# Two products of a projection merged into one of 512 columns, and gate and up columns as units of their own

## The chip, the cores and the metric

The kernel runs on one NeuronCore of a Trainium2 chip. The metric is the device time of one execution in microseconds (us). PE is TensorE (matrix products), PEld its weight loads, DVE is VectorE, ACT is ScalarE, POOL is GpSimd, SP issues the loads of the weights.

## The reference

Two blocks run one after the other, each of two layers, on 256 tokens of width 1024, all in float32. Cut to what matters:

```python
def first_block(x, ...):                       # sequence x alone
    for l in range(2):
        h = rms_norm(x, norm1_g[l])
        rq, rk, rv, rg, sq, sk, sv = split(h @ w_in[l])          # 7 x 512 columns
        ret = head_group_norm(chunk_retention(rotary(rq), rotary(rk), rv)) * silu(rg)
        sb = head_rms_norm(stick_breaking(sq, sk, sv))
        x = x + concat(ret, sb) @ w_out[l]
        h = rms_norm(x, norm2_g[l])
        x = x + (silu(h @ w_gate[l]) * (h @ w_up[l])) @ w_down[l]  # 2816 columns
    return rms_norm(x, final_g)

def second_block(x, c, ctx, c_ctx, ...):       # sequences x and h = ctx, 256 tokens each
    for l in range(2):
        mod_x, mod_h = silu(c) @ w_mod[l] + b_mod[l], silu(c_ctx) @ w_mod[l] + b_mod[l]
        x, h = ffn_sublayer(x, mod_x, 0, ...), ffn_sublayer(h, mod_h, 0, ...)
        # three kinds of mixing between x and h, then w_out
        x, h = ffn_sublayer(x, mod_x, 2, ...), ffn_sublayer(h, mod_h, 2, ...)   # h only if l == 0
    return x

def ffn_sublayer(s, mod, j, g_pre, g_post, wg, wu, wd):
    y = rmsnorm(s, g_pre) * (1 + mod[3*j+1]) + mod[3*j]
    return s + 0.5 * mod[3*j+2] * rmsnorm((silu(y @ wg) * (y @ wu)) @ wd, g_post)
```

## The kernel before, in words

Weights are streamed from memory in pieces of 512 KB (`Gran`), loaded once by SP into `raw` and split into two float32r parts, high and low, in the tile `hl`: for each half of a piece ACT casts the high part and DVE subtracts it to get the low one. Five pieces are held at a time (`R_SLOTS`). Activations are held in the same two parts: `y[:, 0]` is the high part of a normed input, `y[:, 1]` the low one, each as eight slices k of 128 features by 256 tokens. A product is three float32r products that add up in PSUM (`mm3`, L522): weight high by input high, weight high by input low, weight low by input high.

- `proj` (L527) makes two times 128 output features for 256 tokens, in one PSUM bank of two halves: for each slice k, three products of 256 columns for the one piece and three for the other, 48 in all. In block 2's feed-forward and in block 1's, the pair is a gate column and an up column (`col`, L818); in block 1's input projection it is two neighbouring pieces (`rope`, L1098, and `plain`, L1117). Block 2's input projection (`attn2`) uses `proj` too.
- What follows a product is its tail on ACT and DVE. For a column in block 2: silu of the gate half (ACT, tile `sg`), times the up half (DVE), then a split into the parts of `a` (ACT, DVE). In block 1 the factor of each token (`rfac`) is multiplied in first, on both halves (DVE, tile `gu`).
- `row_units` (L760) multiplies two such columns with a 256-row piece of the down weight, in products of 512 columns: into four PSUM banks that are held for the whole feed-forward (`mm_f`), or, for sequence h, into one bank at a time that DVE adds up in SBUF (`mm_r`, `fo`). There are 22 columns and 11 pairs of rows to a feed-forward.
- Ahead of a projection the normed input is turned around by PE (`mm_y`, 16 transposes) and written to `y` by ACT and DVE, slice by slice (`pre_units`, L604, `pre_raw`, L668).
- The modulation of block 2 (`mod_units`, L977) is worked out on DVE beside all this: `modacc` adds up `modraw` times a factor, 1024 columns at a time, loaded by POOL; a total is turned by PE (`mm_t`) and reduced by DVE (`modt`).

The order on PE, DVE and ACT is set by a planner (`run`, L263): it reckons when each instruction starts and ends from a table of costs, issues the products in the order in which they can start, the tails in the order in which they get ready, and puts the modulation wherever DVE is free. That order is fixed in the program; at run time each engine works through its own list and waits for what a step needs. A unit's first product may be ordered 3.5 us ahead of the end of the transposes' tail (`L_TR`).

Of the kernel before, what the change touches and what calls it, by code (L numbers as in the profile page):

```python
# [58 lines left out]
# constant table columns: always on chip, block 1's, block 2's  # L59
# [20 lines left out]
def const_tables():  # L80
    """Tables that depend on shapes alone."""
# [42 lines left out]
class Gran:  # L124
    """A 512 KB piece of a weight: loaded once, split into two float32r parts."""
# [10 lines left out]
# what a unit takes on PE, in ns, and the PSUM banks that it holds until its end  # L136
PE_NS = {"col": 5260, "proj": 5260, "rope1": 5260, "half1": 2630, "half2": 2630, "row": 1295, "row_add": 1295, "row_last": 1295,
# [3 lines left out]
BANKS = {"row": 0, "row_add": 1, "row_last": 0, "half2": 0, "happly": 2, "sc2": 2, "bapply": 2}  # L141
# [6 lines left out]
class Meter:  # L148
    """Reckons when the instructions of DVE and ACT begin and end. at, last: when what the next one needs is
    there, and the engine that it comes from."""  # L150

    def __init__(self):
        self.free = {"v": 0.0, "a": 0.0, "pe": 0.0}
        self.at, self.last = 0.0, None
        self.act_set = None
        self.spawned = []

# [5 lines left out]
    def spawn(self, gen):  # L163
        """gen goes on beside the tail that calls this"""
        self.spawned.append((gen, self.at, self.last))


class Engine:
    """PE, DVE or ACT: issues an instruction and reckons how long it takes."""
# [5 lines left out]
    def ns(self, op, args, kw):  # L175
# [33 lines left out]
class Chained:  # L209
    """DVE, for a short instruction that needs the one before it"""  # L210
# [25 lines left out]
class Tail:  # L236
# [26 lines left out]
def run(streams, grans, r_slots, raw_slots, load, split, meter):  # L263
    """Merges the streams and emits them, at the times that are reckoned: products in the order in which they
    can start, what follows them on DVE and ACT in the order in which it gets ready, and the splitting of
    weights (up to r_slots ahead) and the work on the modulation in between."""
# [28 lines left out]
    def runway():  # L295
        """the work for PE that needs no further piece of a weight; 1e9 if no stream waits for one after it"""
# [37 lines left out]
    def advance(x):  # L334
        meter.at, meter.last = x.at + (CHAIN if x.chained and x.last == "v" else 0.0), x.last
        nxt = next(x.gen, None)
        x.at, x.last = meter.at, meter.last
        u = x.unit
        take_spawned(u)
# [15 lines left out]
    while True:  # L355
        # the next product of each stream
# [102 lines left out]
def tile_two_blocks(ctx: ExitStack, tc, io, out):  # L459
# [40 lines left out]
    def t2k(shape, name):  # L500
        """a short-lived tile of 2 KB per partition"""
        return wk.tile(shape, F32, tag="t2k", name=name, bufs=4)
# [23 lines left out]

    def proj(ps, gs, y, ks=range(KT)):  # L527
        """feature-major: twice 128 output features by 256 tokens"""
# [5 lines left out]
    def proj_t(ps, gp, y, bs=(0, 1)):  # L534
        """token-major: 256 tokens by 256 output features"""
# [6 lines left out]
    def rsqrt_small(v, step=Chained):  # L542
        """v: SBUF [128, n], v > 0; gives v ** -0.5"""
# [24 lines left out]
    def bcast(rb, y):  # L568
        """rb[:, j*128 + t] = y[t, j] on every partition"""
# [4 lines left out]
    def sq_piece(c, b, e, src):  # L574
        """a part of the mean of squares: 512 features of 128 tokens"""
# [7 lines left out]
    def rstd_tok(c, bs, step=Chained, rest=None):  # L583
        """1 / root mean square of the tokens; to come after a yield"""
# [11 lines left out]
    def tail_of(*stages):  # L596
        """a tail from pairs of an engine and what to call"""
# [125 lines left out]
    def post_units(st, c, mode, u, apart=False, final=False, hard=False):  # L723
        """residual plus gate times the norm of what a sublayer gave; apart: one block of tokens at a time"""
# [35 lines left out]
    def row_units(st, c, gp, src_of, first, last, mode, deps, by_token=True):  # L760
        """two feature tiles times [256, 1024] of a weight, token-major: added to the residual ("res"),
        kept in PSUM ("ps") or added up in SBUF ("sb")"""
        u = None
        order = ((0, 0), (0, 1), (1, 0), (1, 1)) if last and by_token else ((0, 0), (1, 0), (0, 1), (1, 1))
        for n_, (b, e) in enumerate(order):
            def fn(b=b, e=e, n_=n_):
# [18 lines left out]
                def tail():  # L785
# [28 lines left out]
    def ffn(st, c, gg, gu, gd, mode, dep, pace, fac=None, by_token=True):  # L814
# [3 lines left out]
        def col(j):  # L818
            def fn():
                y = ytile[c]  # L820
                ps = mm_ps([P, 2, S], "mm_c")
                proj(ps, (gg[j], gu[j]), y)

                def tail():
                    if fac is None:
                        yield A
                        sg = t1k([P, S], "sg")
                        A.activation(sg, ps[:, 0, :], AF.Silu)
                        yield V
                        V.tensor_mul(sg, sg, ps[:, 1, :])  # L830
                    else:
                        yield V, fac["u"]
                        gu_ = t2k([P, 2, S], "gu")
                        sg = gu_[:, 0]
                        V.tensor_mul(gu_, ps, fac["rb"].unsqueeze(1).to_broadcast([P, 2, S]))
                        yield A
                        A.activation(sg, sg, AF.Silu)
                        yield V
                        V.tensor_mul(sg, sg, gu_[:, 1])
# [4 lines left out]
                    A.copy(hl[:, 0, :], sg)  # L844
                    yield V
                    V.tensor_sub(hl[:, 1, :], sg, hl[:, 0, :])
                    abox[j] = hl
                return tail
            cols[j] = st.add("col", fn, grans=[gg[j], gu[j]], deps=dep if j == 0 else ())
            pace.append(cols[j])  # L850

        def row(s):
            def src(k):
# [3 lines left out]
                             [(cols[2 * s + 1], 0.0)], by_token)  # L857

        for j in range(NJ):
            col(j)  # L860
# [13 lines left out]
    def load_rows(ap, n):  # L874
        """n pairs of pieces of 256 rows by 512 columns"""
# [3 lines left out]
    def load_mix(ap, n, kcols):  # L879
        """256-column pieces: pairs by rows for those in kcols, else by columns"""  # L880
# [64 lines left out]
    def start2():  # L945
# [993 lines left out]
```

## Time and profile before

| | |
|---|---|
| median of 3 runs | 2476.24 us (2475.47 to 2477.46) |
| span of the profiled execution | 2474.7 us |
| PE busy | 2415.5 us, 98% |
| DVE busy | 1731.8 us, 70% |
| ACT busy | 1092.0 us, 44% |
| granted TensorE clock, mean | 0.991 of full speed |

The span reaches from the first to the last instruction of the program. Almost all instructions bear the line L205, that of the helper that issues them, so they are told apart by their tiles, in the form out<-in: `mm_c<-y,hl` is a projection's product, `hl<-raw,hl` the second half of a weight's split. The float32 products that are not in two parts run as two passes each in the trace.

### The profile page before, as it was taken

How to read it: one execution, taken by the hardware profiler on the slowest of the kernel's cores; microseconds unless marked ns; L12 is line 12 of the kernel's file. 1: busy time of each engine (PE TensorE's matmuls, PEld its weight loads, DVE VectorE, ACT ScalarE, POOL GpSimd, SP SyncE). 2: the span in 40 equal slices, each digit the busy share in tenths (PEclk: the TensorE clock that was granted, in tenths of full speed). 3: DMA queues.
4: the chain of work that ended last, by engine and by line, in shares of the span. 5: the costliest groups of instructions: out<-in, count | busy, mean ns of one | idle time of the engine just before them, and what ended most of it. 6: DMA issues, size and time to landing. Idle time of an engine off the chain costs nothing.

```text
span 2474.7 us, 42550 instructions
## 1 busy us (share of the span) xinstructions
PE 2415.5 (98%) x16927; PEld 2231.3 (90%) x16927; DVE 1731.8 (70%) x3366; ACT 1092.0 (44%) x2337; POOL 99.1 (4%) x189
## 2 busy tenths in 40 slices
PE   7999999999999999999999999999999999997998
PEld 7999999999999999999669999999999998966997
DVE  5789867798879953755788994348899448486554
ACT  6654456544632222545566222236222226465443
POOL 1000000000001100000000100000110000000000
PEclk9999999999999999999999999999999999998999
DMA  6568655687656633622126762245665335322663
GB/s 218 161 209 246 202 161 164 186 254 222 195 173 200 188 93 99 177 88 86 60 94 204 214 188 79 87 125 180 195 203 172 95 94 175 90 86 77 189 193 121
DMA packets 461448, 386.31 MB, mean 156 GB/s; under 512 B 20512, under 2 KB 392548, under 8 KB 461248
## 3 DMA queue, kind: packets, MB, share of 16 engines
q1 hardware_dynamic: 437424, 299.67, 40.9%
q0 software_dynamic: 23648, 83.77, 10.4%
q8 instruction: 133, 2.18, 0.4%
q14 instruction: 67, 0.55, 0.1%
q10 hardware_dynamic: 176, 0.14, 0.0%
HBM read 382.43 MB, written 1.10 MB: 155 GB/s over the span
## 4 chain that ended last, share of the span: by engine, by line
PE 92%; DVE 5%; ACT 1%; issue 1%; DMA 1%; DVEq 0%; ACTq 0%
PE mm_c L205 59%; PE mm_f L205 18%; PE mm_r L205 7%; PE at_s L205 1%; PE mm_t L205 1%; DVE hl L205 1%; PE at_o L205 1%; PE at_t L205 1%; PE at_c L205 1%; DVE res L205 1%; PE mm_y L205 1%; DVE t L205 1%; PE st_rb L205 1%; DVE sx L205 0%; ACT sq L205 0%
## 5 line engine op out<-in xcount | busy, mean ns | idle before, releaser
L205 PE MATMUL mm_c<-y,hl 128*128 128x256 f32 x11616 | 1435.0, 284 | 8.7 <-DVE y L205 5.4
L205 PEld LDWEIGHTS mm_c<-y,hl 128*128 128x128 f32 x11616 | 1416.2, 192 | 23.8 <-DVE y L205 7.7
L205 ACT CAST hl<-raw 128x512 fp32r<-128x512 f32 x1128 | 646.9, 619 | 813.8 <-PE mm_c L205 460.1
L205 DVE TENSOR_TENSOR hl<-raw,hl 128x512 fp32r<-128x512 f32 x1128 | 735.1, 685 | 308.0 <-ACT hl L205 306.7
L205 PE MATMUL mm_f<-hl,a 128*128 128x512 f32 x1584 | 379.9, 392 | 0.0
L205 PEld LDWEIGHTS mm_f<-hl,a 128*128 128x128 f32 x1584 | 292.1, 188 | 58.1
L205 DVE SCALAR_TENSOR_TENSOR modacc<-modraw,sc,modacc 128x1024 f32<-128x1024 f32 x252 | 311.9, 1277 | 0.0
L205 PE MATMUL mm_r<-hl,a 128*128 128x512 f32 x792 | 192.9, 394 | 0.0
L205 ACT ACTIVATE sg<-mm_c 128x256 f32<-128x256 f32 x154 | 58.6, 380 | 303.2 <-PE mm_c L205 300.5
L205 PEld LDWEIGHTS mm_r<-hl,a 128*128 128x128 f32 x792 | 144.8, 188 | 28.1
L205 DVE TENSOR_TENSOR sg<-sg,mm_c 128x256 f32<-128x256 f32 x154 | 64.1, 416 | 151.4 <-ACT sg L205 150.9
L987 POOL DMA_DIRECT2D modraw<-in_w_mod_dram x144 | 77.0, 536 | 1060.2 <-DVE modacc L205 709.7
L205 PE MATMUL mm_f<-hl,o 128*128 128x512 f32 x480 | 119.4, 399 | 0.0
L205 PE MATMUL mm_c<-hl,y 128*128 128x256 f32 x912 | 113.7, 284 | 0.0
L205 PEld LDWEIGHTS mm_c<-hl,y 128*128 128x128 f32 x912 | 111.0, 192 | 0.3 <-issue 0.3
L205 PEld LDWEIGHTS mm_f<-hl,o 128*128 128x128 f32 x480 | 87.7, 188 | 22.9 <-issue 4.2
L205 DVE TENSOR_TENSOR fo<-fo,mm_r 128x512 f32<-128x512 f32 x120 | 81.9, 683 | 12.9 <-PE mm_r L205 11.5
L205 ACT CAST a<-sg 128x256 fp32r<-128x256 f32 x154 | 62.5, 406 | 31.9 <-DVE sg L205 31.9
L205 DVE TENSOR_REDUCE modt<-mm_t 128x4 f32<-128x512 f32 x72 | 49.3, 685 | 34.1 <-PE mm_t L205 34.0
L205 DVE TENSOR_TENSOR a<-sg,a 128x256 fp32r<-128x256 f32 x154 | 64.4, 418 | 8.0 <-ACT a L205 8.0
L205 DVE TENSOR_REDUCE sx<-at_s 128x1 f32<-128x512 f32 (+1 forms) x72 | 40.7, 596 | 31.7 <-PE at_s L205 31.3
L205 DVE TENSOR_TENSOR gu<-mm_c,rfac 128x512 f32<-128x512 f32 x44 | 30.4, 690 | 41.1 <-PE mm_c L205 40.9
(196 smaller groups left out, 1413.5 us busy)
## 6 DMA issues: line engine op xcount, KB each, us to landing
modraw<-in_w_mod_dram POOLq DMA_DIRECT2D x144, 512.0 KB, 4.8
raw<-in_ffn_w_down_dram SPq DMA_DIRECT2D x100, 512.0 KB, 4.1
raw<-in_ffn_w_gate_dram SPq DMA_DIRECT2D x98, 512.0 KB, 4.7
raw<-in_ffn_w_up_dram SPq DMA_DIRECT2D x98, 512.0 KB, 3.8
raw<-in_w_in_dram SPq DMA_DIRECT2D x92, 512.0 KB, 4.7
raw<-in_w_gate_dram SPq DMA_DIRECT2D x44, 512.0 KB, 5.0
raw<-in_w_up_dram SPq DMA_DIRECT2D x44, 512.0 KB, 4.7
raw<-in_w_down_dram SPq DMA_DIRECT2D x44, 512.0 KB, 4.5
```

Source lines behind the costliest of these rows:

```text
L205: return f(*args, **kw)
L987: G.dma_start(M["raw"][g % len(M["raw"])], wm[k * P:(k + 1) * P, i * D:(i + 1) * D])
```

## The change

A new `wide` makes one 128-feature piece in a bank of its own: for each slice k one product of 512 columns, weight high by both parts of `y` at once, into the two halves of the bank, and one of 256 columns, weight low by `y`'s high part, added into the second half. A new `join` adds the halves up: ACT copies the second one to SBUF, DVE adds the first one to it. `gate` and `up` are units of their own now, each with one bank, one piece and one `join`; `rope` and `plain` run two `wide` in two banks. In block 1 the token's factor is multiplied into the gate alone, and the up half's share of it is applied after the last down product (`fac["r"]`). Block 2's input projection and the token-major projections stay as they were. The planner's table gets new costs (a float32r product is reckoned 13.7 ns above its columns, 1.0 before), a count of banks that a tail gives back early, five tiles `t2k` where there were four, and POOL's descriptor memory is set to 8192 bytes.

```diff
-                return n / 2.4 + 1.0
+                return n / 2.4 + 13.7
...
+        if meter.freed:
+            banks += meter.freed
+            u.keep += meter.freed
...
+    def wide(ps, g, y):
+        for k in range(KT):
+            PE.matmul(ps, wsl(g, 0, k, 0, P), y[:, :, k, :], start=k == 0, stop=False)
+            PE.matmul(ps[:, 1, :], wsl(g, 1, k, 0, P), y[:, 0, k, :], start=False, stop=k == KT - 1)
+    def join(*pairs):
+        yield A
+        for dst, ps in pairs:
+            A.copy(dst, ps[:, 1, :])
+        yield V
+        for dst, ps in pairs:
+            V.tensor_add(dst, ps[:, 0, :], dst)
+            meter.freed += 1
...
-                        V.tensor_add(rpiece(c, b, e), rpiece(c, b, e), ps)
+                        if fac is None:
+                            V.tensor_add(rpiece(c, b, e), rpiece(c, b, e), ps)
+                        else:
+                            V.scalar_tensor_tensor(rpiece(c, b, e), ps, fac["r"][:, b:b + 1], rpiece(c, b, e),
+                                                   op0=ALU.mult, op1=ALU.add)
...
-        def col(j):
+        def gate(j):
             def fn():
-                y = ytile[c]
                 ps = mm_ps([P, 2, S], "mm_c")
-                proj(ps, (gg[j], gu[j]), y)
+                wide(ps, gg[j], ytile[c])
 
                 def tail():
...
+                    cols["gu", j] = t2k([P, 2, S], "gu")
+                    sg = cols["gu", j][:, 0]
+                    yield from join((sg, ps))
+                    if fac is not None:
                         yield V, fac["u"]
...
+                        V.tensor_mul(sg, sg, fac["rb"])
+                    yield A
+                    A.activation(sg, sg, AF.Silu)
+                return tail
+            return st.add("gate", fn, grans=[gg[j]], deps=dep if j == 0 else ())
+
+        def up(j, ug):
+            def fn():
+                ps = mm_ps([P, 2, S], "mm_c")
+                wide(ps, gu[j], ytile[c])
+
+                def tail():
+                    sg, t = cols["gu", j][:, 0], cols["gu", j][:, 1]
+                    yield from join((t, ps))
+                    yield V, ug
+                    V.tensor_mul(t, t, sg)
...
-            cols[j] = st.add("col", fn, grans=[gg[j], gu[j]], deps=dep if j == 0 else ())
+            cols[j] = st.add("up", fn, grans=[gu[j]])
```

On PE, at the start of block 1's first feed-forward (`mm_f<-hl,o` is the end of its mixer, `st_rb` spreads the tokens' factors), before:

```order
L205 MATMUL mm_f<-hl,o_1169 128x512 x60
L205 MATMUL mm_y<-cst,res_78 128x128 x16
L205 MATMUL mm_c<-y_1571,hl 128x256 x48
L205 MATMUL st_rb<-cst,rs_t 128x128 x2
L205 MATMUL mm_c<-y_1571,hl 128x256 x144
L205 MATMUL mm_f<-hl,a_1752 128x512 x24
```

And in the changed kernel, from the same point on:

```order
L207 MATMUL mm_f<-hl,o_1137 128x512 x54
L207 MATMUL mm_y<-cst,res_78 128x128 x16
L207 MATMUL mm_c<-y_1465,hl 128x512
L207 MATMUL mm_c<-y_1465,hl 128x256
L207 MATMUL mm_c<-y_1465,hl 128x512
L207 MATMUL mm_c<-y_1465,hl 128x256
L207 MATMUL mm_c<-y_1465,hl 128x512
L207 MATMUL mm_c<-y_1465,hl 128x256
```

Products of 512 and of 256 columns alternate now, and the first gate unit alone, 16 products, stands where a whole column of 48 stood behind the transposes.

On DVE, in the same feed-forward, shortly ahead of the first reduction of a modulation total (`modacc` is the modulation, `a` the last step of a column's tail), before:

```order
L205 TENSOR_TENSOR gu<-mm_c,rfac 128x512
L205 TENSOR_TENSOR hl<-raw,hl 128x512 x2
L205 TENSOR_TENSOR gu<-gu 128x256
L205 TENSOR_TENSOR hl<-raw,hl 128x512 x2
L205 TENSOR_TENSOR a_1752<-gu,a_1752 128x256
L205 SCALAR_TENSOR_TENSOR modacc<-modraw,sc,modacc 128x1024
```

And in the changed kernel, at the same place:

```order
L207 TENSOR_TENSOR gu<-mm_c,gu 128x256
L207 TENSOR_TENSOR gu<-gu,rfac 128x256
L207 TENSOR_TENSOR hl<-raw,hl 128x512
L207 SCALAR_TENSOR_TENSOR modacc<-modraw,sc,modacc 128x1024
L207 TENSOR_TENSOR gu<-mm_c,gu 128x256
L207 TENSOR_TENSOR gu<-gu 128x256
L207 TENSOR_TENSOR hl<-raw,hl 128x512 x2
L207 TENSOR_TENSOR a_1652<-gu,a_1652 128x256
L207 SCALAR_TENSOR_TENSOR modacc<-modraw,sc,modacc 128x1024
```

A column has five short steps on DVE in block 1, where it had one of 512 columns and two of 256, and the modulation's steps stand closer together between the splits.

## Rows read from the trace of the kernel before

**Rows 1.** The page: busy time by engine, and the chain by engine.
```profile
PE 2415.5 (98%) x16927; PEld 2231.3 (90%) x16927; DVE 1731.8 (70%) x3366; ACT 1092.0 (44%) x2337; POOL 99.1 (4%) x189
...
PE 92%; DVE 5%; ACT 1%; issue 1%; DMA 1%; DVEq 0%; ACTq 0%
```

**Rows 2.** Groups: line, engine, operation, names, shapes, count | busy us, mean ns | idle before.
```profile
L205 PE MATMUL mm_c<-y,hl 128*128 128x256 f32 x11616 | 1435.0, 284 | 8.7 <-DVE y L205 5.4 <-ACT hl L205 1.4 <-DVE hl L205 1.1
...
L205 DVE TENSOR_TENSOR sg<-sg,mm_c 128x256 f32<-128x256 f32 x154 | 64.1, 416 | 151.4 <-ACT sg L205 150.9
...
L205 DVE TENSOR_TENSOR gu<-mm_c,rfac 128x512 f32<-128x512 f32 x44 | 30.4, 690 | 41.1 <-PE mm_c L205 40.9
...
L205 ACT ACTIVATE sg<-mm_c 128x256 f32<-128x256 f32 x154 | 58.6, 380 | 303.2 <-PE mm_c L205 300.5 <-issue 2.7
```

**Rows 3.** Timeline of PE, late feed-forward: start us, us, instruction, shape, count.
```profile
2301.94 5.63 PE L205 MATMUL mm_f<-hl,a 128*128 128x512 f32 x24
2307.41 11.68 PE L205 MATMUL mm_c<-y,hl 128*128 128x256 f32 x96
2318.92 0.63 PE L205 MATMUL mm_f<-hl,a 128*128 128x512 f32 x2
```

**Rows 4.** Timeline of PE, block 2: a run of 48 of 512 columns.
```profile
2055.10 11.07 PE L205 MATMUL mm_r<-hl,a 128*128 128x512 f32 x48
2066.01 0.40 PE L205 MATMUL mm_c<-y,hl 128*128 128x256 f32 x2
```

**Rows 5.** Timeline of PE, then DVE, start of block 1's first feed-forward.
```profile
148.94 6.21 PE L205 MATMUL mm_c<-y,hl 128*128 128x256 f32 x48
154.99 0.60 PE L205 MATMUL st_rb<-cst,rs_t 128*128 128x128 f32 x4
...
150.05 2.44 DVE L205 SCALAR_TENSOR_TENSOR y<-mm_y,vecs,y 128x256 fp32r<-128x256 f32 x6 [0.46 <-ACT y L205]
```

**Rows 6.** Timeline of PE, then DVE, block 2's first feed-forward of x.
```profile
678.96 23.18 PE L205 MATMUL mm_c<-y,hl 128*128 128x256 f32 x191 [0.85 <-DVE y L205]
...
682.80 0.61 DVE L205 TENSOR_SCALAR y<-t,modt 128x256 fp32r<-128x256 f32 x2
```

**Rows 7.** Timeline of PE, then DVE, block 2's last feed-forward of x.
```profile
2277.67 24.44 PE L205 MATMUL mm_c<-y,hl 128*128 128x256 f32 x192
2301.94 0.86 PE L205 MATMUL mm_f<-hl,a 128*128 128x512 f32 x3
...
2281.27 0.61 DVE L205 TENSOR_SCALAR y<-t,modt 128x256 fp32r<-128x256 f32 x2
```

**Rows 8.** Timeline of PE, second layer of block 2, from h to x.
```profile
1699.00 12.17 PE L205 MATMUL mm_c<-y,hl 128*128 128x256 f32 x96
1713.34 3.75 PE L205 MATMUL mm_y<-cst,z 128*128 128x128 f32 x16 [2.17 <-DVE z L205]
```

**Rows 9.** Timeline of DVE, block 1's first feed-forward.
```profile
180.29 3.67 DVE L205 SCALAR_TENSOR_TENSOR modacc<-modraw,sc,modacc 128x1024 f32<-128x1024 f32 x3
...
201.11 0.69 DVE L205 TENSOR_TENSOR gu<-mm_c,rfac 128x512 f32<-128x512 f32 x1 [1.05 <-PE mm_c L205]
201.72 1.28 DVE L205 TENSOR_TENSOR hl<-raw,hl 128x512 fp32r<-128x512 f32 x2
202.92 0.41 DVE L205 TENSOR_TENSOR gu<-gu 128x256 f32<-128x256 f32 x1
203.25 1.28 DVE L205 TENSOR_TENSOR hl<-raw,hl 128x512 fp32r<-128x512 f32 x2
```

**Rows 10.** Timeline of DVE: a total's reduction.
```profile
1498.80 0.69 DVE L205 TENSOR_REDUCE modt<-mm_t 128x4 f32<-128x512 f32 x1 [4.25 <-PE mm_t L205]
1499.53 0.17 DVE L205 TENSOR_TENSOR modt<-modt,vecs 128x4 f32<-128x4 f32 x1
1499.61 0.42 DVE L205 TENSOR_TENSOR sg<-sg,mm_c 128x256 f32<-128x256 f32 x1
```

**Rows 11.** Busy time by engine in two stretches with modulation and one without.
```profile
core 0: us, PE busy (x) PEld busy (x) DVE busy (x) ACT busy (x) POOL busy (x), PEclk, DMA share, GB/s
223.65:287.63 63.98, 63.98 (x450) 60.03 (x449) 56.43 (x87) 29.16 (x59) 2.64 (x5) 1.00 0.77 230
730.21:884.99 154.78, 154.78 (x1123) 146.43 (x1122) 137.74 (x200) 39.87 (x86) 15.60 (x29) 1.00 0.61 187
917.00:1017.00 100.00, 100.00 (x713) 94.51 (x712) 41.16 (x75) 29.27 (x63) 0.00 (x0) 1.00 0.34 100
```

More of the change, by code (lines that the diff above doesn't have):

```diff
@@ L133, in __init__ @@
         self.hl = None
-PE_NS = {"col": 5260, "proj": 5260, "rope1": 5260, "half1": 2630, "half2": 2630, "row": 1295, "row_add": 1295, "row_last": 1295,
+PE_NS = {"gate": 2780, "up": 2780, "proj": 5560, "projt": 5760, "rope1": 5560, "half1": 2880, "half2": 2880,
+         "row": 1365, "row_add": 1365, "row_last": 1365,
          "tr": 450, "total": 440, "put": 110, "rbc": 430, "start1": 30, "start2": 300, "r1": 650, "r2": 650, "r3": 430,
@@ L156, in __init__ @@
         self.spawned = []
+        self.freed = 0
     def op(self, e, ns):
@@ L334, in advance @@
     def advance(x):
+        nonlocal banks
         meter.at, meter.last = x.at + (CHAIN if x.chained and x.last == "v" else 0.0), x.last
+        meter.freed = 0
         nxt = next(x.gen, None)
@@ L500, in t2k @@
     def t2k(shape, name):
-        return wk.tile(shape, F32, tag="t2k", name=name, bufs=4)
+        return wk.tile(shape, F32, tag="t2k", name=name, bufs=5)
     def t1k(shape, name):
@@ L758, in coef_unit, with row_units @@
         st.add("none", fn, deps=[(mod_done[l, j], 0.0)])
-    def row_units(st, c, gp, src_of, first, last, mode, deps, by_token=True):
+    def row_units(st, c, gp, src_of, first, last, mode, deps, by_token=True, fac=None):
         u = None
@@ L856, in row @@
             return row_units(st, c, gd[s], src, s == 0, s == NJ // 2 - 1, mode,
-                             [(cols[2 * s + 1], 0.0)], by_token)
+                             [(cols[2 * s + 1], 0.0)], by_token, fac)
         for j in range(NJ):
-            col(j)
+            up(j, gate(j))
             if j >= 3 and j % 2 == 1:
@@ L1096, in block1_layer, with pair @@
         ev = {}
+        def pair(gi):
+            pss = [mm_ps([P, 2, S], "mm_c") for _ in range(2)]
+            for ps, g in zip(pss, gw[gi]):
+                wide(ps, g, ytile[X])
+            return pss
         def rope(name, gi):
             def fn():
-                ps = mm_ps([P, 2, S], "mm_c")
-                proj(ps, gw[gi], ytile[X])
+                pss = pair(gi)
                 def tail():
-                    yield V, fac["u"]
                     hb = gi % 2
                     dst = B[name][:, 2 * hb:2 * hb + 2, :]
+                    s = t2k([P, 2, S], "rs")
+                    yield from join(*((s[:, i, :], pss[i]) for i in range(2)))
+                    yield V, fac["u"]
                     t2 = t2k([P, 2, S], "rt")
                     cos = fac["cos"].unsqueeze(1).to_broadcast([P, 2, S])
-                    V.tensor_mul(dst, ps, cos)
+                    V.tensor_mul(dst, s, cos)
                     for a, b in ((0, 64), (64, 0)):
                         sn = fac["sin"][b:b + 64].unsqueeze(1).to_broadcast([64, 2, S])
-                        V.tensor_mul(t2[a:a + 64], ps[b:b + 64], sn)
+                        V.tensor_mul(t2[a:a + 64], s[b:b + 64], sn)
                     V.tensor_add(dst, dst, t2)
@@ L1120, in fn @@
                     alloc1()
-                ps = mm_ps([P, 2, S], "mm_c")
-                proj(ps, gw[gi], ytile[X])
+                pss = pair(gi)
                 def tail():
-                    yield V, fac["u"]
                     hb = gi % 2
                     dst = B[name][:, 2 * hb:2 * hb + 2, :]
+                    yield from join(*((dst[:, i, :], pss[i]) for i in range(2)))
+                    yield V, fac["u"]
                     rb = fac["rb"].unsqueeze(1).to_broadcast([P, 2, S])
                     if scale != 1.0:
-                        V.scalar_tensor_tensor(dst, ps, scale, rb, op0=ALU.mult, op1=ALU.mult)
+                        V.scalar_tensor_tensor(dst, dst, scale, rb, op0=ALU.mult, op1=ALU.mult)
                     else:
-                        V.tensor_mul(dst, ps, rb)
+                        V.tensor_mul(dst, dst, rb)
                     if name == "rg":
@@ L1158, in block1_layer @@
         for fn, gi, nm in order:
-            ev[nm] = sx.add("rope1" if nm[:2] in ("rk", "rq") else "proj", fn, grans=gw[gi], deps=first)
+            kind = "rope1" if nm[:2] in ("rk", "rq") else "projt" if nm[:2] in ("rv", "sv") else "proj"
+            ev[nm] = sx.add(kind, fn, grans=gw[gi], deps=first)
             first = ()
```

23 lines of the change are left out of this document (5 added, 18 removed).

## The prediction

> **What bounds the kernel now.** I read the page first, then the groups of instructions, then the timelines of PE and DVE, then busy time by stretch. The page shows PE busy for 98% of the span and on 92% of the chain that ended last; DVE is at 70%, ACT at 44% [rows 1]. So a change is worth what it takes from PE's own list, less the time for which PE is made to wait. The largest group on PE is the projection's product of 256 columns, 11616 of them [rows 2]; its mean of 284 ns is no cost, since the records of pipelined matmuls overlap. What one costs is the distance between starts. In the timeline 96 of them stand between 2307.41 and 2318.92 us, so one takes 11.51 / 96 = 119.9 ns. The 24 products of 512 columns ahead take 2307.41 - 2301.94 = 5.47 us, 227.9 ns each [rows 3], and a run of 48 takes 2066.01 - 2055.10 = 10.91 us [rows 4]. From 24 to 48 it grows by 5.44 us, so one more costs 226.7 ns. At 2.4 GHz, the granted clock being 1.00 in the stretches I looked at [rows 11], 256 columns are 106.7 ns and 512 are 213.3. So each product carries about 13 ns that don't depend on its width. That is what the change can save.
>
> **The products.** 396 units of gate and up and 40 pieces in block 1's input projection become `wide`: 436 pieces of 8 slices, 3488 slices. They take 3 x 3488 = 10464 of the 11616 products; the other 1152 are block 2's input projection. A slice cost 3 x 119.9 = 359.7 ns; it will cost 227.9 + 119.9 = 347.8, 11.9 less. 3488 x 11.9 ns = **-41.5 us**. Two things in it have no row: a moving operand in two pieces (`y[:, :, k, :]`), and a change of width at every product. The best price is 226.7 + 119.9 = 346.6, 13.1 saved, -45.7 us. For the worst I take the bounds of a change of width: the runs of 24 and 48 put it between nothing and 24 x (227.9 - 226.7) = about 26 ns, if all of the excess of a short run falls on its beginning; then a slice costs 346.6 + 26 = 372.7, +13.0, or +45 us. I stay near the cheap end, since the 96 that follow a change back pay none of it [rows 3], and an excess that small over a whole run is nearer to the modelled ends than to a stall of every product.
>
> **The first unit behind a transpose.** Products of a column may start before `y` is whole, but can't end before its last slice is written. A column is 48 x 119.9 ns = 5.76 us, the first gate unit only 8 x 347.8 ns = 2.78 us, so it hides less of that writing. It can't end sooner than some 0.06 us of handoff and one slice's 0.35 us behind the last write. In block 1's first feed-forward the last write ends at 152.49 and the column, begun at 148.94, ended at 154.99 [rows 5]. After, the gate ends at 152.9 at the earliest, and up behind it at 152.9 + 2.78 = 155.7, where 154.99 less the two units' saving of 16 x 11.9 ns = 0.2 gives 154.8: 0.9 us lost. In block 2's first the last write ends at 683.41 and the first column ended at 678.96 + 5.76 = 684.7 [rows 6]; after, 683.8 + 2.78 = 686.6 against 684.5, 2.1 lost. In its last the write ends at 2281.88, the column at 2277.67 + 5.76 and a little waiting, 2283.8 [rows 7]; after, 2282.3 + 2.78 = 2285.1 against 2283.6, about 1.5 lost. Three such places in block 1 between nothing and 0.9 make about 2 us, four in block 2 between 1.5 and 2.1 about 7: **+9 us**. Sequence h's feed-forward has work of the down product ahead of these places and pays nothing.
>
> **A hole that is filled.** At 1713.34 PE waited 2.17 us for DVE's `z` [rows 8]. Two columns (11.5 us) stood ahead; in the new order five half units (13.9 us) do: **-2 us**.
>
> **DVE beside the modulation.** The planner puts the modulation wherever it thinks DVE is free. It reckoned a product 12.7 ns too short, about 12% of a 256-column one, so it left DVE slack without knowing. With the true cost it packs tighter. Of the two stretches with modulation in the rows, DVE was busy 56.43 of 63.98 us and 137.74 of 154.78, 88 and 89%; without modulation it is at 41% [rows 11]. After, I count the new order's instructions between the same totals and price them by starts: a split 0.60 to 0.64, `modacc` 1.2 (3.67 for three), 256 columns 0.33 to 0.41, 512 from PSUM 0.61 [rows 9], a reduction 0.73 + 0.08 [rows 10]. In the first stretch 36 splits, 14 `modacc`, 30 short steps and 4 reductions make 21.7 + 16.7 + 10.0 + 3.2 = 51.7 us, against 51.1 of PE. In the second it is 144.7 against 145.0. Over all five such stretches DVE has some 504 us of work and PE some 503. DVE then runs at PE's pace with nothing to spare, and what is queued behind a late `modacc` on DVE is a split that PE's products wait for. What covers it: five pieces held, down rows two columns behind the columns, four banks, so some 5 us of lag per stretch, and it recovers where the modulation ends. Bounds: nothing with full cover; 504 / 0.97 - 503 = 17, say 20 us, if DVE can't be kept busier than 97%; 504 / 0.88 - 503 = 70 if it stays at the share it has now. A small loss in each of five stretches, **+7 us**, is what I take, nearer to the covered end.
>
> **At nothing, with its cover.** The joins add 436 copies on ACT (380 ns each, 166 us, to 51%) and 436 adds on DVE (416 ns, 181 us; less 44 x (690 - 416) ns = 12 us in block 1) [rows 2], so DVE goes to about 1900 us, 78%. Outside the modulation's stretches both have room. The last column's tail grows by a copy and an add, to some 2.1 us with its split and handoffs; the 24 down products ahead of the last rows take 5.47 us [rows 3] and hide it; uncovered it would be about 0.8 us for each of nine feed-forwards. The factor at the last down row changes one DVE instruction for another of the same size. A smaller descriptor memory touches POOL, 4% busy [rows 1]; its loads wait for DVE to give back `modraw`, and a late one would add to the DVE term.
>
> **Sum.** 2474.7 - 41.5 + 9 - 2 + 7 = 2447.2 us of span. The median stands 1.5 us above the span of the profiled execution, so 2448.7, **2449 us**.
>
> **A page that speaks against it.** The products march at 119.9 and 227.9 ns [rows 3], which leaves 13 ns above the columns at either width. The Trainium skill ("TensorE: Matmul & The Clock Gate", section "Back-to-back issue gap") gives the isolated gap of a warm product as its columns over 2.4 GHz plus 2.5 ns. By it, a product saved would be worth 3488 x 2.5 ns = 8.7 us, an estimate from that page, and the junctions and DVE would eat all of it. The trace disagrees at both widths, and the sum goes by the trace.
>
> **The rivals.**
> 1. *DVE at its limit, mildly.* The cushions don't hold, and DVE runs at 97% in the five stretches: +20 in place of +7, 2462 us. For it: the work of the two engines is equal. Against: before, nothing of the order of microseconds was lost to DVE outside the places behind transposes; PE idled 8.7 us ahead of all 11616 products, 5.4 of it for `y` [rows 2]. Chance 0.15.
> 2. *DVE becomes the bound: slower.* DVE's 88% may be what its waits on ACT, on PSUM and on `modraw` let through, and no slack. Then 504 us of work take 573 and PE waits 70 us in those stretches: 2474.7 - 41.5 + 9 - 2 + 70 + 1.5 = 2512 us. The gain without the DVE term is 34.5 us, so it decides from a share of 504 / 537.5 = 94% down. For it: the longer chain from bank to `a` (PE, ACT, DVE, DVE, ACT, DVE). Against: in the timeline DVE goes from step to step without gaps but for one `gu` [rows 9]. Chance 0.10.
> 3. *The change doesn't save what it says.* The two-piece operand or the change of width costs the 12 ns again: 2474.7 + 9 - 2 + 7 + 1.5 = 2490 us. For it: no row shows either. Against: the run of 96 right behind a change of width [rows 3]. Chance 0.07.
> 4. *All of it is kept.* 13.1 ns a slice (-45.7), cushions and early starts hide the rest: 2474.7 - 45.7 + 1.5 = 2430 us. Chance 0.08.
>
> **How the numbers follow.** The forecast keeps 0.60, within 2438 to 2459 (the DVE term between 0 and 17, the junctions between 5 and 13, the products to -45.7). From 2430 to 2470 the range takes in rival 1 and the better half of rival 4: 0.60 + 0.15 + 0.05 = 0.80. A measurement of this kernel can tell about 0.2%, 5 us. The forecast and rivals 1 and 4 are faster than that, 0.83. Rivals 2 and 3 are slower, 0.17; some 0.05 of it falls within 5 us of the time before, where a mechanism is only half as dear: same 0.05, slower 0.12.
>
> **What would show it.** Right: runs of 16 products at 2.78 us in the late feed-forward; a wait of the first gate unit on DVE's `y` of 1 to 2 us at the places of [rows 5 to 7]; no hole before `z`; DVE at 95% and more in the modulation's stretches with few waits of PE there; DVE near 1900 us, ACT near 1260. Wrong: a run of 16 at 2.88 us (rival 3), or PE waiting for `hl` or `mm_c`'s banks for tens of microseconds in those stretches (rivals 1 and 2).

## The result, and the profile after

The changed kernel takes 2491.32 us (median of 4 runs, 2487.04 to 2492.46), the kernel before 2476.85 in the same session: a ratio of 1.0055, 95% interval 1.0043 to 1.0067. It is slower by 14.5 us where 27 us less was forecast, and it lies outside the range. The profiled execution has a span of 2488.8 us, 14.1 more than the 2474.7 of before.

The page of the changed kernel: busy time by engine, and the chain by engine (against [rows 1]).

```profile
PE 2406.5 (97%) x13439; PEld 2049.7 (82%) x13439; DVE 1882.4 (76%) x3802; ACT 1257.3 (51%) x2775; POOL 99.2 (4%) x189
...
PE 68%; DVE 9%; ACT 2%; issue 1%; DMA 1%; DVEq 0%; ACTq 0%
```

The 3488 products are gone (16927 - 13439), and DVE and ACT stand near the forecast (1900 and 1260). But PE's busy time fell by 9 us only while the span grew, so PE stands idle more. The second line can't be set against that of before: its shares add up to 81%, since this chain is followed back to 472 us of the span only.

The late feed-forward on PE, start and duration in us, with the count behind x (against [rows 3]; a group bears the shape of its first product, so x64 are 32 of 512 and 32 of 256 columns):

```profile
2317.72 5.63 PE L207 MATMUL mm_f<-hl,a 128*128 128x512 f32 x24
2323.18 11.45 PE L207 MATMUL mm_c<-y,hl 128*128 128x512 f32 x64
2334.47 5.67 PE L207 MATMUL mm_f<-hl,a 128*128 128x512 f32 x24
```

32 slices march in 2334.47 - 2323.18 = 11.29 us, 352.8 ns a slice. Before, the same work took 11.51 us, 359.7 ns a slice [rows 3]. The slice saves 6.9 ns, not 11.9: 24 us over 3488 slices, not 41.5.

So the rest, 14 + 24 = 38 us, was lost by waiting. One sum over the whole trace agrees: I took each distance between two starts on PE and subtracted the median distance of products of the same name and shape. What is left over is 87.2 us before and 126.4 after, +39. In what follows this sum is called **the stalls**. It also holds the products that ran at the lower clock, and it comes from one execution of each kernel, the profiled one.

PE's waits in the changed kernel: who waited for whom, us in total, times, longest.

```profile
PE mm_y L207 <- DVE z L207: 21.5, 8, 10.8
...
PE mm_c L207 <- DVE y L207: 8.5, 16, 1.5
...
PE mm_c L207 <- DVE hl L207: 5.5, 2, 5.3
...
PE mm_f L207 <- ACT a L207: 2.3, 2, 1.4
```

Before, products waited 5.4 us for `y` and 1.1 for `hl` [rows 2], and transposes 16.2 for `z`:

```profile
PE mm_y L205 <- DVE z L205: 16.2, 4, 10.5
```

What has been added is many small waits and one of 5.3 us. The wait of 10.8 us was there before, as 10.5. The down products (`mm_f`) waited for neither `a` nor `o` before; now it is 2.3 us for `a` and 2.5 for `o`.

### The profile page after: what moved, and what is told of

It reads as the page before. It is cut to its first block, busy times and chain, and to the rows that moved or that the text cites. A ratio compares the mean times of both kernels' runs of the same rounds, so it can differ in the third digit from the quotient of the medians.

```text
span 2488.8 us, 36605 instructions
## 1 busy us (share of the span) xinstructions
PE 2406.5 (97%) x13439; PEld 2049.7 (82%) x13439; DVE 1882.4 (76%) x3802; ACT 1257.3 (51%) x2775; POOL 99.2 (4%) x189
## 4 chain that ended last, share of the span: by engine, by line
PE 68%; DVE 9%; ACT 2%; issue 1%; DMA 1%; DVEq 0%; ACTq 0%
PE mm_c L207 43%; PE mm_f L207 13%; PE mm_r L207 6%; DVE hl L207 2%; PE at_s L207 1%; PE mm_t L207 1%; ACT sq L207 1%; DVE t L207 1%; PE at_t L207 1%; DVE res L207 1%; PE at_c L207 1%; DVE gu L207 1%; PE at_o L207 1%; ACT hl L207 1%; PE mm_y L207 0%
## 5 line engine op out<-in xcount | busy, mean ns | idle before, releaser
L207 PE MATMUL mm_c<-y,hl 128*128 128x512 f32 (+1 forms) x8128 | 1417.9, 333 | 16.3 <-DVE y L207 8.5
L207 PEld LDWEIGHTS mm_c<-y,hl 128*128 128x128 f32 x8128 | 1222.2, 190 | 189.6 <-issue 8.1
L207 DVE TENSOR_TENSOR hl<-raw,hl 128x512 fp32r<-128x512 f32 x1128 | 743.7, 686 | 292.0 <-ACT hl L207 290.7
L207 ACT CAST hl<-raw 128x512 fp32r<-128x512 f32 x1128 | 668.4, 620 | 504.8 <-PE mm_c L207 276.3
L207 DVE TENSOR_TENSOR gu<-mm_c,gu 128x256 f32<-128x256 f32 x396 | 165.6, 418 | 113.9 <-ACT gu L207 113.3
L207 ACT COPY gu<-mm_c 128x256 f32<-128x256 f32 x396 | 145.3, 368 | 151.8 <-PE mm_c L207 151.7
L207 ACT CAST a<-gu 128x256 fp32r<-128x256 f32 x198 | 80.6, 407 | 191.9 <-DVE gu L207 191.8
L207 ACT ACTIVATE gu<-gu 128x256 f32<-128x256 f32 x198 | 82.7, 419 | 147.2 <-DVE gu L207 146.8
L207 DVE TENSOR_TENSOR a<-gu,a 128x256 fp32r<-128x256 f32 x198 | 83.0, 419 | 14.6 <-ACT a L207 14.6
L207 DVE TENSOR_TENSOR gu<-gu 128x256 f32<-128x256 f32 x198 | 83.9, 424 | 5.4
```

Of the source, the lines that this page charges most:

```text
L207: return f(*args, **kw)
```

## The experiments

All ratios are against the kernel before, run on the same chip between the others.

### Where the other 5 ns of a slice went

Two things had no row: the operand in two pieces, and the change of width. The first run takes the pieces away (the same edit stands in two places):

```diff
-                    ytile[c] = wk.tile([P, 2, KT, S], F32R, tag=f"y{c}", name=f"y{c}")
+                    ytile[c] = wk.tile([P, KT, 2, S], F32R, tag=f"y{c}", name=f"y{c}").rearrange("p k h s -> p h k s")
```

> The changed kernel with y laid out so that the two parts of a slice lie side by side: the moving operand of a 512-column product is one piece, in the same order of instructions. In the changed kernel a pair of 512 and 256 columns marches at about 351.9 ns (64 products, 32 pairs, in 2334.47 - 2323.18 = 11.29 us), not at 347.8. If the two pieces cost the 4 ns, a pair takes 347.8 ns here and the kernel is 3488 x 4.1 ns = 14 us faster than the changed one, 2477 us. If they cost nothing, 2491 us as before the edit, and the march stays at 352.

2491.95 us, ratio 1.0054 (1.0039 to 1.0069). The march on PE there:

```profile
2321.56 11.45 PE L207 MATMUL mm_c<-y,hl 128*128 128x512 f32 x64
2332.85 5.44 PE L207 MATMUL mm_f<-hl,a 128*128 128x512 f32 x23
```

Again 11.29 us. A moving operand in two pieces costs nothing that this shows. (11.29 us for 32 pairs is 352.8 ns a pair; the expectations write 351.9, and so 3.5 ns where the change of width comes out as 4.4 below.)

The second run puts equal widths together:

```diff
         for k in range(KT):
             PE.matmul(ps, wsl(g, 0, k, 0, P), y[:, :, k, :], start=k == 0, stop=False)
+        for k in range(KT):
             PE.matmul(ps[:, 1, :], wsl(g, 1, k, 0, P), y[:, 0, k, :], start=False, stop=k == KT - 1)
```

> The changed kernel with the eight 512-column products of a piece first and the eight 256-column ones behind them: two changes of width in a piece where there were sixteen. If a change of width costs the 4 ns of a pair, 32 pairs march at 11.13 us where they took 11.29, and the kernel takes 2491 - 14 x 7/8 = 2479 us. If it doesn't, the march stays at 11.29 us. At the first gate unit the low products now stand behind all the high ones, which changes the place of the wait but hardly its end: within 3 us.

2493.74 us, ratio 1.0061 (1.0046 to 1.0076): no faster. But the march is:

```profile
2324.75 11.31 PE L207 MATMUL mm_c<-y,hl 128*128 128x512 f32 x64
2335.90 1.32 PE L207 MATMUL mm_f<-hl,a 128*128 128x512 f32 x5
```

11.15 us, 348.4 ns a slice, close to the 347.8 of the prediction. So the change of width does cost, about 4.4 ns a slice, and the kernel didn't get the gain: its stalls are 142.4 us against 126.4. In the first gate unit all eight low products now stand behind the last slice of `y`, and in most of the stretches that begin with transposes the stalls grew, by up to some 4 us. My expectation said that this would hardly move the end; it did.

### What the merge is worth, and what came with it

```diff
-            PE.matmul(ps, wsl(g, 0, k, 0, P), y[:, :, k, :], start=k == 0, stop=False)
+            PE.meter.op("pe", 512 / 2.4 + 13.7)
+            for h in range(2):
+                nc.tensor.matmul(ps[:, h, :], wsl(g, 0, k, 0, P), y[:, h, k, :], start=k == 0 and h == 0, stop=False)
```

The planner is charged as for the merged product, so the order is the same.

> The changed kernel with each 512-column product undone into two of 256 columns, in the same planned order, banks and tails: the merge alone taken back. If a pair saves the 7.8 ns that the march shows (359.7 - 351.9), this takes 27 us longer than the changed kernel, 2518 us; by the 11.9 ns of the prediction it would be 41 us, 2532. If it is no slower than 2500, the merge saves nothing, and what the changed kernel lost isn't a matter of stalls beside it.

2510.85 us, ratio 1.0132 (1.0117 to 1.0148). The merge is worth 2510.9 - 2491.3 = 19.5 us between medians (spans: 2511.8 - 2488.8 = 23), somewhat under the 24 to 27 of the march. And the changed kernel without its merge stands 33 us behind the kernel before. The prediction had 9 - 2 + 7 = 14 us for all of that. The next runs divide the 33.

**The planner's cost.** One line in each of two kernels: the old cost in the changed one, and this, the new cost in the one before.

```diff
-                return n / 2.4 + 1.0
+                return n / 2.4 + 13.7
```

> The changed kernel with the planner's former cost of a product, 1.0 ns above its columns, and all else as changed. By the prediction's term for DVE (the planner now packs the modulation as tight as PE's time allows, 7 us lost), this is 2484 us with longer stretches of modulation and DVE under 90% in them. If the packing costs nothing, as the few waits of PE for hl in the changed kernel say, 2489 to 2495 us.

2490.43 us, ratio 1.0062 (1.0046 to 1.0079): no different from the changed kernel.

> The kernel before with the planner's new cost of a product alone (13.7 ns above its columns). If the tighter packing of the modulation costs PE anything, this is slower than before by some of the predicted 7 us: 2480 to 2485. If it costs nothing, 2478 us, and the 33 us that the changed kernel lost with its products undone (2510.9 against 2478.0) come from the units and their tails.

2474.26 us, ratio 0.9988 (0.9978 to 0.9997): 3 us faster than before, if anything. So the tighter packing costs nothing there. In the changed kernel it did come: these are the two stretches of modulation of the changed kernel that answer to [rows 11] (us, busy time and count of PE, PEld, DVE, ACT, POOL, granted clock, DMA share, GB/s).

```profile
220.30:273.40 53.10, 53.10 (x287) 45.44 (x286) 52.55 (x89) 26.29 (x58) 2.63 (x5) 1.00 0.75 231
732.40:879.90 147.50, 147.50 (x799) 126.25 (x798) 145.06 (x229) 51.98 (x116) 15.31 (x29) 1.00 0.63 190
```

DVE is busy for 99 and 98% of them, near the 51.7 and 144.7 us that the prediction counted, and PE is busy all of the time. In all five stretches together (166 to 271, 489 to 594, 697 to 877, 1358 to 1504 and 1746 to 1926 us) DVE is busy for 709.9 of 716 us, and PE's stalls are 2.4 us. The old cost, which I had expected to leave DVE under 90%, left it at 97 and 95% (112.45 of 116 us, 170.92 of 180), so that part of my expectation was wrong too, and that run says little about the packing.

**The joins.** Whole columns again (gate and up in one unit with two banks and one tail), with the merge and, in a second kernel, without it (there with the edit to two products of 256 as well). The unit is cut to its products and its joins:

```diff
+        def col0(j):
+            def fn():
+                pss = [mm_ps([P, 2, S], "mm_c") for _ in range(2)]
+                y = ytile[c]
+                for k in range(KT):
+                    for ps, g in zip(pss, (gg[j], gu[j])):
+                        PE.matmul(ps, wsl(g, 0, k, 0, P), y[:, :, k, :], start=k == 0, stop=False)
+                        PE.matmul(ps[:, 1, :], wsl(g, 1, k, 0, P), y[:, 0, k, :], start=False, stop=k == KT - 1)
...
+                    yield from join((sg, pss[0]), (t, pss[1]))
...
-            up(j, gate(j))
+            col0(j)
```

> The changed kernel with gate and up of every column in one unit again (two banks, one tail with both joins, merged products slice by slice in turn): the merge without the split into units. If the split is what costs (the short first unit, the filler that runs out at half columns, the loads that slip behind coef), what is left is the kernel before with the new cost (2474) less the 27 us of the march: 2447 to 2455 us, and the waits behind the transposes are those of before. If the stalls come from the joins and the longer tails, 2475 to 2485 us.

2472.69 us, ratio 0.9980 (0.9971 to 0.9990): 18.6 us less than the changed kernel, but far from the 2447 to 2455 us of the split as the only cause, and 2 us under the 2475 to 2485 of the joins. Something else of some 20 us is left, and the next kernel says what.

> Whole columns as in the kernel with gate and up in one unit again, in the same planned order, with each 512-column product undone into two of 256: the banks, joins and tails of the change without its merge and without its split. Against the kernel before with the new cost (2474.3 us) it has only the joins and the second bank more. If these cost the stalls that whole columns still show (105 us above the march against 86), this is 2474.3 + 19 = 2493 us, and the merge alone is worth 2493 - 2472.7 = 20 us there. If the joins are covered, as the prediction took them to be, it stands at 2476 to 2480 and the merge is worth only 3 to 8 us with whole columns.

2494.89 us, ratio 1.0072 (1.0056 to 1.0089). This kernel differs from the one before with the new cost by the joins, the longer tails and the second bank, with the small edits that came along (the planner's table of units, block 1's factor, a fifth `t2k`, POOL's descriptor memory) and an order that is planned as for merged products. It stands 2494.9 - 2474.3 = 20.6 us behind it. Its stalls are 105.3 us against 86.2. The 19 us are spread over some fifteen stretches, none with more than some 4.

Two kinds of wait among them are no chain from a join to PE. In the stretches of modulation PE waits seven times, 3.5 us in all, for DVE's reduction of a total: at 240.01 us the first product of an up piece stands until the reduction has ended at 239.86, so the column's second bank is short there. The changed kernel, with one bank to a unit, has no wait of `mm_c` for `modt`.

```profile
240.01 0.47 PE L894 MATMUL mm_c<-y,hl 128*128 128x256 f32 x2 [0.54 <-DVE modt L207]
```

And at the end of each of block 1's mixers PE waits 1.27 us for ACT's `o`, since ACT's list has a weight's cast ahead of that of `o`; the changed kernel has these two waits too. The rest stands mostly behind norms (waits for `z`, `y` and the tokens' factors), more at some and less at others. One place where PE waits for the norm of sequence x; first the kernel before with the new cost, then this one (start, us, instruction, idle before):

```profile
1059.01 5.92 PE L205 MATMUL mm_c<-hl,y 128*128 128x256 f32 x48
1065.81 2.16 PE L205 MATMUL mm_y<-cst,z 128*128 128x128 f32 x16 [0.88 <-DVE z L205]
```

```profile
1071.99 5.92 PE L207 MATMUL mm_c<-hl,y 128*128 128x256 f32 x48
1080.15 3.72 PE L207 MATMUL mm_y<-cst,z 128*128 128x128 f32 x16 [2.25 <-DVE z L207]
```

The hole is 1.4 us longer, and the transposes behind it took 3.72 us in place of 2.16. (In the kernel before without the new cost this hole was 1.76 us.) Which instruction on DVE or ACT is late at each such place was not isolated. That the joins and what came with them cost 20.6 us is shown; how much of it is the copies and adds alone is not.

**The split into units.** By the same kernels it costs 2510.9 - 2494.9 = 16.0 us without the merge and 2491.3 - 2472.7 = 18.6 with it. (Without the merge, the whole columns wait 3.5 us for the second bank and the halves don't, so by that the split's own waits are more than the 16.0.) Two parts of it could be taken out one by one. The first edit, with `col0` as above for the first column alone:

```diff
-            up(j, gate(j))
+            if j == 0:
+                col0()
+            else:
+                up(j, gate(j))
```

> The changed kernel with the gate and the up piece of the first column of each feed-forward in one unit, slice by slice in turn, as the kernel before had them (merged products, two banks, one tail). If the short first gate unit costs what the prediction says, the wait behind the transposes shrinks by 1 to 2 us at each of the seven feed-forwards without cover, and the time is 2491 - 9 = 2482 us. If the losses at those places come from late z and y and not from the unit's length, 2489 to 2491 us.

2486.0 us, ratio 1.0034 (1.0021 to 1.0046): 5.3 us less than the changed kernel, between the two expectations. Its six executions lie between 2476.3 and 2488.4 us, so the 5.3 is good to some 4. The short first unit costs, by the medians less than 9. The edit leaves block 1's input projections alone, whose first unit begins with a single piece too. Its place in the changed kernel, block 2's first feed-forward of x on PE (against [rows 6]):

```profile
681.25 1.91 PE L207 MATMUL mm_y<-cst,z 128*128 128x128 f32 x16
684.64 0.94 PE L207 MATMUL mm_c<-y,hl 128*128 128x512 f32 x4 [1.49 <-DVE y L207]
685.95 0.95 PE L207 MATMUL mm_c<-y,hl 128*128 128x512 f32 x4 [0.37 <-DVE y L207]
687.25 0.94 PE L207 MATMUL mm_c<-y,hl 128*128 128x512 f32 x4 [0.36 <-DVE y L207]
688.57 3.71 PE L207 MATMUL mm_c<-y,hl 128*128 128x512 f32 x20 [0.38 <-DVE y L207]
```

The gate unit is done four products at a time, as DVE writes `y`: the mechanism is the one predicted, with 2.6 us of waits in four pieces.

The other part was in no step of the prediction. In the changed kernel, POOL's queue and PE between the mixer and the second feed-forward of h in block 2's first layer (the idle time is in brackets):

```profile
1325.76 0.54 POOL L780 DMA_DIRECT2D coef<-coefd  x1 [47.00 <-DVE mm_f L207]
1326.29 2.08 POOL L1019 DMA_DIRECT2D modraw<-in_w_mod_dram  x4
```

```profile
1326.75 0.37 SPq L1935 DMA_DIRECT2D raw<-in_ffn_w_gate_dram  x1
...
1330.35 4.99 SPq L1935 DMA_DIRECT2D raw<-in_ffn_w_gate_dram  x1
...
1338.59 0.62 ACT L207 CAST hl<-raw 128x512 fp32r<-128x512 f32 x1 [8.54 <-DMA raw<-in_ffn_w_gate_dram]
```

```profile
1323.58 11.69 PE L207 MATMUL mm_c<-y,hl 128*128 128x512 f32 x65
1340.59 5.06 PE L207 MATMUL mm_c<-y,hl 128*128 128x256 f32 x15 [5.32 <-DVE hl L207]
1347.86 3.85 PE L207 MATMUL mm_y<-cst,z 128*128 128x128 f32 x16 [2.21 <-DVE z L207]
```

The first four loads of the next layer's modulation, 512 KB each, stand in POOL's queue behind the load of `coef`, which waits for the mixer's end on DVE. Then they go out together, just as SP loads weights of the feed-forward. The gate piece that SP issued in their midst, at 1326.75, lands 11.8 us later; ACT's cast waits 8.54 us for it, and PE 5.32 us for its split. (With the edit below, the same piece lands after 6.1 us.) SP's next gate piece takes 4.99 us to be issued, 0.37 elsewhere; that is not the piece that PE waits for. Before, the four went out from 1274.96 to 1285.01 us, ahead of that `coef`:

```profile
1285.01 0.53 POOL L987 DMA_DIRECT2D modraw<-in_w_mod_dram  x1 [1.98 <-PE at_t L205]
1335.47 0.53 POOL L987 DMA_DIRECT2D modraw<-in_w_mod_dram  x1 [49.93 <-DVE modacc L205]
1335.99 0.53 POOL L757 DMA_DIRECT2D coef<-coefd  x1
```

The order on POOL turned around: the planner began this modulation later (its first step on DVE is at 1358.1 us, before at 1333.8), and its loads with it. In the edit `open_` takes the buffers and issues the first four loads, as a step of its own:

```diff
+        if l == 1 and lo == 0:
+            smod.add("none", open_, deps=[(pace, 0.0)] + after)
```

> The changed kernel with the first four loads of the second layer's modulation put on POOL's queue as soon as their buffers are free, ahead of the load of coef that waits for DVE's mm_f; nothing else moves. In the changed kernel the four stand behind that load, go out together at 1326.29 us beside the weights, a gate piece lands 8.5 us late and PE stands for 5.3 us at 1335, then runs its next transposes and products at the lower clock. If that is a loss of its own, 2491.6 - 5.3 - 4 to 7 = 2479 to 2482 us, and no wait of PE for hl is left. If the late piece had another cause, 2491.

2484.8 us, ratio 1.0034 (1.0023 to 1.0045): 6.5 us less than the changed kernel, where 9 to 12 had been expected. PE at the same place:

```profile
1323.58 14.24 PE L207 MATMUL mm_c<-y,hl 128*128 128x512 f32 x80
1342.18 3.86 PE L207 MATMUL mm_y<-cst,z 128*128 128x128 f32 x16 [4.37 <-DVE z L207]
```

The wait for `hl` is gone, but 2.2 us of the 5.3 went to the next thing that was late, `z`. Before, PE had three columns (144 products, 17.4 us) to do there and no wait at all for `z`; now it has five half units (80 products, 14.1 us), since a sixth was issued ahead of the last down products. This is the filler of [rows 8] the other way around.

### Together

> The kernel with all three edits less the grouped order: the first column in one unit and the early loads, widths in turn in all pieces. If the grouped order is worth the 3.5 ns a pair by itself, 2470.3 + 9 to 12 = 2479 to 2482 us, which is also 2491.6 - 5.6 - 6.8 by the two edits alone. If those two add to more when they are together, 2470 to 2474 us.

The first column in one unit and the early loads, with no other edit: 2479.55 us, ratio 1.0009 (0.9999 to 1.0018). The two edits add up as expected.

> The changed kernel with three edits: the first column's gate and up in one unit, slice by slice; the eight 512-column products ahead of the eight 256-column ones in all other pieces; the early loads of the modulation. If a change of width costs 3.5 ns a pair (351.9 against 348.4 when grouped) and the grouped order lost it again only behind the transposes, where the first column now goes slice by slice: 2491.6 - 5.6 (first column) - 11 (loads) - 12 (3488 x 3.5 ns) = 2463 us. If the grouped order loses elsewhere, 2475.

The same with the grouped order as well: 2470.33 us, ratio 0.9972 (0.9962 to 0.9981), between the two expectations. Against the kernel without the grouped order it is 9.2 us faster: grouped widths do pay once the first column goes slice by slice.

> As the kernel with whole columns, but in every column except a feed-forward's first the eight 512-column products of a piece stand ahead of its eight 256-column ones, and the first loads of the second layer's modulation go out early. If the change of width costs 3.5 ns a pair, this is some 3300 x 3.5 = 11 us faster than the whole columns in turn: 2436 to 2444 us if those take 2447 to 2455. If the grouped order gains nothing by itself, the same time as whole columns in turn.

Whole columns in the grouped order, the first of each feed-forward slice by slice, with the early loads: 2455.19 us, ratio 0.9909 (0.9893 to 0.9926): 22 us faster than the kernel before, the best of all, but not the 2436 to 2444 expected, which rested on whole columns at 2447 to 2455. It is 17.5 us faster than whole columns in turn, where the march accounts for some 15. Its late feed-forward on PE:

```profile
2306.38 11.31 PE L207 MATMUL mm_c<-y,hl 128*128 128x512 f32 x64
2317.53 5.63 PE L207 MATMUL mm_f<-hl,a 128*128 128x512 f32 x24
```

11.15 us for 32 slices again. Its stalls are 106.8 us, still 20 more than in the kernel before, about the joins' part.

## Why the prediction was wrong

The medians divide the result as follows; it starts from 2476.9 to 2478.0 us, as the kernel before measured in the sessions. The intervals of the ratios are 2 to 4 us to each side, so a step is good to some 4 us.

| step, from one kernel to the next | predicted | measured |
|---|---|---|
| new cost in the planner (modulation packed tight) | +7 | -3 |
| joins, longer tails, second bank | 0 | +20.6 |
| split into gate and up units | +9 - 2 | +16.0 |
| merged products | -41.5 | -19.5 |
| sum | -27.5 | +14 |

- **The step that failed first is "at nothing, with its cover".** I costed the joins at nothing because ACT would be at 51% and DVE at 78% over the whole span. The shares came out right (51 and 76%), the conclusion did not: the joins and what came with them cost 20.6 us, spread over the span. Some 6 us of it are waits for the second bank (3.5 us, which the changed kernel's halves don't have) and for `o` (2.5 us); the rest is mostly where PE waits for a chain on DVE and ACT. I had reckoned the cover at one place only, the end of a feed-forward, and it doesn't hold there either in the changed kernel. At 1047 us 27 down products (6.2 us) stood ahead, and PE still waited 1.41 us for `a`: on ACT the last column's two copies came only 4.8 us behind its last product, after a cast that waited 3.80 us for a weight and the four squares of a norm.

```profile
1041.68 0.62 ACT L207 CAST hl<-raw 128x512 fp32r<-128x512 f32 x1 [3.80 <-DMA raw<-in_ffn_w_down_dram]
...
1044.67 0.62 ACT L207 COPY gu<-mm_c 128x256 f32<-128x256 f32 x2
...
1047.59 1.15 PE L207 MATMUL mm_f<-hl,a 128*128 128x512 f32 x3 [1.41 <-ACT a L207]
```

- **The products: right mechanism, wrong size.** The saving in the march is 6.9 ns a slice and not 11.9; a run of 16 takes 2.82 us, between the 2.78 of the forecast and the 2.88 of rival 3. The prediction had named the change of width as unknown, with a bound from a run of 24 against one of 48; it took the cheap end because a run of 96 showed no excess. That run has one change of width, the changed kernel one at every product. (The bound's 24 x (227.9 - 226.7) ns is 29 and not 26; the forecast doesn't use it.) Grouping brought the march back to 348.4 ns, the contiguous operand did not: it is the alternation. The Trainium skill ("TensorE: Matmul & The Clock Gate", section "Back-to-back issue gap") gives an isolated warm product 2.5 ns above its columns, by which undoing the merge would cost 8.7 us, an estimate from that page. The trace doesn't agree: undoing it cost 19.5. The price of [rows 3] holds for products of one width, 348.4 ns a slice against the 347.8 predicted.
- **The short first unit and the filler: the sign right, the sum too small.** The gate unit waits where I said. But taking it out of the feed-forwards gave 5.3 us and the whole split cost 16 to 19. In the difference are the loads that slipped behind `coef` (6.5 us) and the filler that ran out at 1342 us; the hole of [rows 8] shrank to 0.57 us between two starts, but at 1050 and at 1708 the transposes start 2.03 us behind the down product ahead of them, where it had been 0.23, and those down products had waited 1.41 and 0.89 us for `a`. What the rest of the split's cost is made of was not isolated. I had looked at POOL's share of 4%, and not at what stands in front of what in its queue.
- **DVE beside the modulation.** The count of work was right to 2%, the cost was not: PE lost 2.4 us in all five stretches, at 98 to 99% of DVE, no more than before. Rivals 1 and 2 are refuted.
- **Rival 3 had the time, 2490 us, but not the cause.** It let the whole saving vanish and kept the small losses; in fact half of the saving stayed, and the losses were more than twice as large. A time that agrees proves no mechanism.
- The range was too narrow in one direction: it had bounds for the price of a product and for DVE, and none for the step that I had set to zero.

## What to carry to other kernels

Merge products by their columns, but keep equal widths next to each other, and keep the unit behind a transpose as long as it was. A low busy share over the span doesn't show that a short step added to every tail is covered: ask at each place where PE waits for a chain what the step does there, or leave out the merge and measure the step alone. After each change of order look at the queue of the loads as well: here a load that waited for another engine held up four behind it, and then they went out at once.

## What had not been expected of the hardware

- Products of 512 and 256 columns in turn take 352.8 ns a pair, in groups of eight 348.4. In the changed kernel the median distance behind a start is 235 ns for 512 columns and 118 for 256; in groups it is 228 and 120. Why the wide one takes 7 ns more and the narrow one 2 less was not found.
- A wait of PE can cost more than its length. The granted clock of three stretches in the changed kernel (the columns as above): transposes at 681.3 us behind products without a pause, at 2290.1 us behind a wait of 10.82, and at 1348 behind one of 2.21, where the products ahead, behind the wait of 5.32, had run at 0.50 already.

```profile
681.30:683.10 1.80, 1.80 (x17) 1.61 (x15) 1.15 (x3) 1.38 (x4) 0.00 (x0) 1.00 1.02 416
2290.10:2293.50 3.40, 3.40 (x16) 3.13 (x16) 1.35 (x5) 2.38 (x6) 0.00 (x0) 0.50 0.45 154
1348.00:1351.50 3.50, 3.50 (x16) 3.10 (x16) 3.47 (x8) 3.50 (x9) 0.00 (x0) 0.50 0.73 203
```

  The clock is 1.00 in the first (2.4 GHz) and 0.50 in the others (1.2 GHz), and the 16 transposes take 1.91 us in the one and 3.77 to 3.85 in the others, some 1.9 more. The length of the last wait doesn't decide alone. In the changed kernel two sets of transposes stand behind waits of the same length:

```profile
1070.79 2.16 PE L207 MATMUL mm_y<-cst,z 128*128 128x128 f32 x16 [1.54 <-DVE z L207]
...
1705.36 1.15 PE L207 MATMUL mm_f<-hl,a 128*128 128x512 f32 x3 [0.89 <-ACT a L207]
1708.03 3.71 PE L207 MATMUL mm_y<-cst,z 128*128 128x128 f32 x16 [1.53 <-DVE z L207]
```

  The first ran at a clock of 1.00, the second, with another wait shortly ahead, at 0.55.
- DVE can stand at 99% for 53 us and at 98% for 147 beside a PE that is never idle.
